# A layer's feed-forward: its first three output pairs as plain products of a low and a high token half, placed in a written order beside the making of their operands

## Chip, cores, metric

One core of one Trainium2 chip. The time is device microseconds of one execution; the figure for a kernel is the median of its runs.

## What is computed

A decoder layer on 512 tokens of width 2048: a modulated RMS norm, one projection into a short convolution and an attention group, an output projection with a gated residual, a second modulated norm, a feed-forward of width 8192 with squared ReLU, a gated residual, a last norm. The change lies between the end of the output projection and the first pairs of the feed-forward:

```
x = x + g1 * ([RMSNorm(y_conv) | RMSNorm(y_nsa)] @ W_out)
h = RMSNorm(x) * (1 + scale2) + shift2
x = x + g2 * (relu(h @ W1)^2 @ W2)
return RMSNorm(x)
```

## The kernel before, in words

Everything is float32. A product in full precision is three TensorE matmuls of operands that are each split into a high and a low part of the type float32r: high by high, high by low, low by high (`mm3`, lines 92 to 95). ScalarE makes the high part by a copy, VectorE the low part by a subtraction (`split`, `hilo`, `tsplit`). A weight block is 128 x 1024; `hilo` (line 794) is thus one operation of 1024 columns on each of the two engines.

**The end of the output projection.** Eight blocks of `w_oa2` are made into `kept` (lines 829 to 840). `late_out(hf)` (line 843) multiplies them with one half of the tokens (256 columns): eight products of 24 matmuls, and after each the gated residual (line 809), a square on ScalarE (line 804) and its sum on VectorE (line 805). Low half and high half together are 16 late products.

**Tokens.** When the sums of a half are complete, `row_norm` and `row_bcast` (lines 168 to 183) make the reciprocal root of each token and spread it over the partitions, with two small matmul steps. `normed` (line 872) multiplies by it on VectorE (tile xr) and modulates on ScalarE (line 880). `low_tokens` splits the low half into the token tiles B1 and B2; `high_tokens(q)` takes the high half, forms with the low half the differences and sums of a Strassen scheme of seven products, and splits those (tiles tk).

**The feed-forward.** The first matrix has 32 output pairs (256 columns of W1 each); a pair has four blocks, a11, a21, a22, a12. `ff1(p)` (line 966) makes seven products in place of eight: `operands` (line 913) forms the four sums of blocks that the scheme needs (VectorE, 1024 columns each, lines 917, 918, 930, 932), and splits seven operands; each product is `run`: 24 matmuls of 256 columns. The results are added up on VectorE and ScalarE, and seven tiles of the next layer's operands are split and stored to DRAM through the GpSimd queue (lines 1001 to 1014). The seven products in order are B1, U6, T5, B2, T7, B3, T4. Two of them, B1 and B2, need low tokens alone. So `ahead` (line 957) makes B1 and B2 for pairs 0 to 2 early, between the steps of `high_tokens`; these six products are left out when the pair's turn comes, which leaves five a pair.

**Order.** The program is written with a scheduler that may move instructions of one engine past each other where data allow it; `pin` keeps those passed to it in written order while `pinned[0]` is True. In the kernel before that is so only in the first part (lines 98 to 406). In the stretch of the change the scheduler chooses the order. Each engine then runs its own list strictly in that order, waiting at semaphores for others.

**Buffers that matter.** Three tiles `hl` for split blocks; six `rw` for raw blocks, loaded by the SyncE queue; three `gt` and one `gb` for what is stored to DRAM, each free again only when its stores have landed; eight PSUM banks; five small `t` tiles.

## Time and profile before

| | |
|---|---|
| median of 3 runs | 2225.86 us (2222.83 to 2229.16) |
| profiled execution, its own time | 2224.18 us |
| its span, first to last instruction | 2222.4 us |
| granted TensorE clock, mean | 0.982 |

The profile is of one execution. PE is TensorE's matmuls, PEld its weight loads, DVE VectorE, ACT ScalarE, POOL GpSimd, SP SyncE. A row of the timeline has the start and the length in microseconds, the engine, the line, the operation, the tiles written and read with their shape, a count, and in brackets the idle time ahead of it and what ended it. A row of busy time by stage has the window, its width, the busy time of each engine with the number of instructions, the granted clock, the DMA share and GB/s.

### The profile page before, as it was taken

To read this page: it belongs to the slowest core of one execution; us is meant where nothing else is said; L and a number is where in the kernel's file an instruction comes from. 1 tells how busy PE (TensorE), PEld (TensorE's weight loads), DVE (VectorE), ACT (ScalarE), POOL (GpSimd) and SP (SyncE) were. 2 spreads that over 40 slices of the span, in tenths; PEclk is the share of its full clock that TensorE was granted. 3 is DMA by queue.
4 is the path that set the end of the run, shared out by engine and by line. 5 is a ranking of instruction groups with operands and counts; after the bars stand their busy time and mean duration, and the time that the engine had idled before them with its cause. 6 is when DMAs were issued, how large, how long until landed. Compare 5 with 4: busy or idle time off the path is not lost.

```text
span 2222.4 us, 37638 instructions
## 1 busy us (share of the span) xinstructions
PE 2133.1 (96%) x14942; PEld 1971.6 (89%) x14942; DVE 1918.5 (86%) x2998; ACT 1008.6 (45%) x1468; POOL 193.6 (9%) x366
## 2 busy tenths in 40 slices
PE   6999999999999999799999999999899999999996
PEld 4777778898777779799999999999899999999996
DVE  8889988877496687999999999999898999999996
ACT  4432333223354425565666655666333333333353
POOL 0000000000000001021111111113111011001100
PEclk8999999999999999799999999999999999999998
DMA  8985687864211174276665666658865366356432
GB/s 351 336 321 187 235 302 269 348 233 162 81 39 67 48 286 164 83 235 209 199 203 189 198 209 204 204 187 285 298 237 210 141 237 237 129 214 247 168 118 95
DMA packets 143985, 453.62 MB, mean 204 GB/s; under 512 B 15809, under 2 KB 20161, under 8 KB 143809
## 3 DMA queue, kind: packets, MB, share of 16 engines
q1 hardware_dynamic: 92192, 323.27, 40.6%
q0 software_dynamic: 51616, 127.95, 17.3%
q8 instruction: 117, 1.92, 0.3%
q14 instruction: 60, 0.48, 0.1%
HBM read 383.00 MB, written 68.16 MB: 203 GB/s over the span
## 4 chain that ended last, share of the span: by engine, by line
PE 77%; DVE 13%; ACT 5%; DMA 3%; issue 2%; SPq 0%; POOL 0%; DVEq 0%; ACTq 0%; POOLq 0%
PE pf L95 19%; PE pf L93 19%; PE pf L94 18%; PE ps L95 5%; PE ps L94 5%; PE ps L93 5%; DVE scr L134 3%; DVE wl L84 2%; DVE hl L796 1%; ACT wh L83 1%; PE pw L94 1%; PE pw L95 1%; PE pw L93 1%; PE pt L714 1%; PE pv L93 1%
## 5 line engine op out<-in xcount | busy, mean ns | idle before, releaser
L93 PE MATMUL pf<-tk,hl 128*128 128x256 f32 x3576 | 1008.8, 282 | 11.5 <-ACT hl L795 9.1
L95 PE MATMUL pf<-tk,hl 128*128 128x256 f32 x3576 | 1006.2, 282 | 11.4 <-DVE hl L796 11.4
L94 PE MATMUL pf<-tk,hl 128*128 128x256 f32 x3576 | 1007.7, 282 | 1.3 <-DVE tk L867 1.3
L93 PEld LDWEIGHTS pf<-tk,hl 128*128 128x128 f32 x3576 | 678.7, 190 | 14.9 <-ACT hl L795 12.0
L95 PEld LDWEIGHTS pf<-tk,hl 128*128 128x128 f32 x3576 | 677.6, 190 | 14.0 <-DVE hl L796 13.9
L94 PEld LDWEIGHTS pf<-tk,hl 128*128 128x128 f32 x3576 | 677.5, 189 | 1.6 <-DVE tk L867 1.6
L795 ACT ACTIVATE hl<-rw 128x1024 fp32r<-128x1024 f32 x264 | 278.9, 1056 | 299.2 <-PE pf L95 253.2
L796 DVE TENSOR_TENSOR hl<-rw,hl 128x1024 fp32r<-128x1024 f32 x264 | 321.9, 1219 | 28.8 <-ACT hl L795 28.6
L795 ACT ACTIVATE hl<-sg 128x1024 fp32r<-128x1024 f32 x189 | 200.3, 1061 | 269.2 <-PE pf L95 245.6
L796 DVE TENSOR_TENSOR hl<-sg,hl 128x1024 fp32r<-128x1024 f32 x189 | 230.6, 1221 | 41.9 <-ACT hl L795 41.5
L134 DVE SCALAR_TENSOR_TENSOR scr<-wa,cs 128x1024 bf16<-128x1024 f32 x176 | 210.9, 1220 | 5.9 <-DMA wa<-in_w_ada 5.6
L83 ACT ACTIVATE wh<-raw 128x1024 fp32r<-128x1024 f32 (+1 forms) x105 | 110.9, 1060 | 223.6 <-PE ps L94 105.1
L84 DVE TENSOR_TENSOR wl<-raw,wh 128x1024 fp32r<-128x1024 f32 (+1 forms) x105 | 128.6, 1225 | 57.8 <-ACT wh L83 56.8
L870 DVE TENSOR_TENSOR sg<-sg,rw 128x1024 f32<-128x1024 f32 x126 | 153.6, 1219 | 0.9
L95 PE MATMUL ps<-h_m,wl 128*128 128x512 f32 x360 | 142.8, 397 | 2.4 <-DVE wl L84 2.4
L93 PE MATMUL ps<-h_m,wh 128*128 128x512 f32 x360 | 142.6, 396 | 1.8 <-DVE part L384 1.0
L94 PE MATMUL ps<-h_m,wh 128*128 128x512 f32 x360 | 141.8, 394 | 0.0
L1044 DVE SCALAR_TENSOR_TENSOR x<-pf,mod,x 128x256 f32<-128x256 f32 x256 | 120.1, 479 | 15.3 <-PE pf L95 12.3
L93 PE MATMUL ps<-h,wh 128*128 128x512 f32 x280 | 113.4, 405 | 12.6 <-ACT wh L83 8.9
L95 PE MATMUL ps<-h,wl 128*128 128x512 f32 x280 | 113.6, 406 | 2.4 <-DVE wl L84 2.4
L94 PE MATMUL ps<-h,wh 128*128 128x512 f32 x280 | 113.0, 404 | 0.0
L1010 POOL DMA_DIRECT2D g<-gt x192 | 101.0, 532 | 86.5 <-DVE gt L867 81.6
(314 smaller groups left out, 2972.6 us busy)
## 6 DMA issues: line engine op xcount, KB each, us to landing
rw<-in_w_f SPq DMA_DIRECT2D x262, 512.0 KB, 4.4
wa<-in_w_ada SPq DMA_DIRECT2D x176, 512.0 KB, 5.9
tk<-g POOLq DMA_DIRECT2D x114, 512.0 KB, 8.9
g<-gt POOLq DMA_DIRECT2D x192, 256.0 KB, 5.0
raw<-in_w_conv SPq DMA_DIRECT2D x32, 512.0 KB, 6.2
g<-gb POOLq DMA_DIRECT2D x36, 256.0 KB, 2.3
raw<-in_w_kv SPq DMA_DIRECT2D x16, 512.0 KB, 5.4
raw<-in_w_cv SPq DMA_DIRECT2D x16, 512.0 KB, 4.3
```

Of the source, the lines that this page charges most:

```text
L83: pin(nc.scalar.activation(wh[:, :cols], raw[:, :cols], AF.Copy))
L84: pin(nc.vector.tensor_tensor(out=wl[:, :cols], in0=raw[:, :cols], in1=wh[:, :cols].bitcast(F32), op=OP.subtract))
L93: pin(nc.tensor.matmul(ps, lh, rh, start=start, stop=False, skip_group_check=more))
L94: pin(nc.tensor.matmul(ps, lh, rl, start=False, stop=False, skip_group_check=more))
L95: pin(nc.tensor.matmul(ps, ll, rh, start=False, stop=stop, skip_group_check=more))
L134: pin(nc.vector.scalar_tensor_tensor(out=scr, in0=w, scalar=1.0, in1=cs[i].rearrange("p a b -> p (a b)"), op0=OP.mult, op1=OP.mult, accum_ ...
L714: nc.tensor.transpose(pt[:, r * P:(r + 1) * P], probs[b, r][:, kb * P:(kb + 1) * P], ident)
L795: nc.scalar.activation(dst[0], src, AF.Copy)
L796: nc.vector.tensor_tensor(out=dst[1], in0=src, in1=dst[0].bitcast(F32), op=OP.subtract)
L870: nc.vector.tensor_tensor(out=dst, in0=x, in1=y, op=op)
L1010: nc.gpsimd.dma_start(out=gd[p // 4][idx[j]][p % 4 // 2][:, p % 2], in_=g[:, j])
L1044: nc.vector.scalar_tensor_tensor(out=xm, in0=src, scalar=gate, in1=xm, op0=OP.mult, op1=OP.add)
```

## The change

In the whole kernel, calls are wrapped in `pin`, which changes nothing where `pinned[0]` is False. Between the making of `kept` and pair 3 it is now True, and the order is written out:

- The late products get half a bank each. Each residual is issued one product later.
- `norm_steps`, `low_tokens` and `high_tokens` are generators that yield after each piece the VectorE time that its author gives it, or None where the next piece belongs between two products.
- `product` issues one product, then the making of the operands listed for it, then pieces from the generators until their clock has caught up with 2.82 a product.
- Pairs 0 to 2 are computed without Strassen sums: four blocks by two token halves, 24 products of the same size where there were 21. `plan` lists them: the low half for pairs 0, 1, 2 (A11 and A21 with B1, A12 and A22 with B2), then the high half for pairs 2, 0, 1 (tokens T5 and B3). A product of the high half goes on in the other half of the same bank, whose low result was copied (`snapshot`). The high half of T5 is now x_high - x_low, so the accumulated high half plus the copy gives the result.
- `makes` says after which product an operand is made, `stay` which operands are kept for the second half; 19 blocks are split in these pairs, where there were 21.
- `outcome(p)` is the end of a pair: Relu, Square, the sums for the next layer and the stores, again as a generator. What is still waiting after product 24 is issued in full before pair 3 begins.
- In pairs 3 to 31 the tokens of T5 have the other sign, so one block of seven is made negated (`hilo(..., minus)`).

The diff, without lines that only gain `pin`:

```
-    def hilo(dst, src):
-        nc.scalar.activation(dst[0], src, AF.Copy)
-        nc.vector.tensor_tensor(out=dst[1], in0=src, in1=dst[0].bitcast(F32), op=OP.subtract)
+    def hilo(dst, src, minus=False):
+        if minus:
+            pin(nc.scalar.activation(dst[0], src, AF.Copy, scale=-1.0))
+            pin(nc.vector.scalar_tensor_tensor(out=dst[1], in0=src, scalar=-1.0, in1=dst[0].bitcast(F32),
+                                               op0=OP.mult, op1=OP.subtract))
+        else:
+            pin(nc.scalar.activation(dst[0], src, AF.Copy))
+            pin(nc.vector.tensor_tensor(out=dst[1], in0=src, in1=dst[0].bitcast(F32), op=OP.subtract))
         return dst
...
-    pm = [bankf() for _ in range(8)]
-    def late_out(hf):
+    late = {}
+    def late_product(hf, i):
+        if i % 2 == 0:
+            late[hf, i] = bankf()
+        ps = late[hf, i - i % 2][:, halves[i % 2]]
+        wh, wl = kept[i]
+        for k in range(8):
+            s = slice(k * P, (k + 1) * P)
+            mm3(ps, wh[:, s], wl[:, s], mixa[k][:, 0, halves[hf]], mixa[k][:, 1, halves[hf]], k == 0, k == 7)
+    def late_residual(hf, i):
         c = halves[hf]
-        for i in range(8):
-            wh, wl = kept[i]
-            for k in range(8):
-                s = slice(k * P, (k + 1) * P)
-                mm3(pm[i][:, c], wh[:, s], wl[:, s], mixa[k][:, 0, c], mixa[k][:, 1, c], k == 0, k == 7)
-            residual(pm[i], 8 + i, c)
-            if i % 2:
-                j = 4 + i // 2
-                nc.gpsimd.dma_start(out=x1d[j][:, :, c], in_=x1[j][:, :, c])
+        residual(late[hf, i - i % 2][:, halves[i % 2]], 8 + i, c)
+        if i % 2:
+            j = 4 + i // 2
+            pin(nc.gpsimd.dma_start(out=x1d[j][:, :, c], in_=x1[j][:, :, c]))
...
+    def norm_steps(hf):
+        total = bankf()
+        yield None
+        for t in range(2):
+            pin(nc.tensor.matmul(total[:, t:t + 1], sacc[:, (2 * hf + t) * P:(2 * hf + t + 1) * P], ones[:, 0:1],
+                                 start=True, stop=True))
+        rs = small.tile([P, NQ], F32, name="rs")[:, :2]
+        pin(nc.scalar.activation(rs, total[:, :2], AF.Sqrt, scale=1.0 / D, bias=eps))
+        yield 0.0
+        pin(nc.vector.reciprocal(rs, rs))
+        dg = temp([P, 2, P], name="dg")
+        pin(nc.vector.tensor_tensor(out=dg, in0=ident[:, None, :].to_broadcast([P, 2, P]),
+                                    in1=rs[:, :, None].to_broadcast([P, 2, P]), op=OP.mult))
+        yield 0.6
+        ps = bankf()
+        yield None
+        pin(nc.tensor.matmul(ps[:, :HT], ones, dg.rearrange("p a b -> p (a b)"), start=True, stop=True))
+        pin(nc.scalar.activation(r2[:, halves[hf]], ps[:, :HT], AF.Copy))
+        yield 0.0
     def low_tokens():
-        row_norm(bankf, sacc, D, r2, 0, 2)
+        for i in (B1, B2):
+            for q in range(4):
+                tok[i][q] = tslot()
+        def parts(i, u, kp):
+            dst = tok[i][kp // 2][:, kp % 2]
+            return dst, x1[kp][:, u, LO]
...
+        for kp in range(9):
+            if kp < 8:
+                normed(kp, 0)
+                yield 0.6
+            if kp:
+                dst, x = parts(B1, 0, kp - 1)
+                pin(nc.vector.tensor_tensor(out=dst[:, 1], in0=x, in1=dst[:, 0].bitcast(F32), op=OP.subtract))
+                yield 0.35
+            if kp < 8:
+                for u, i in ((0, B1), (1, B2)):
+                    dst, x = parts(i, u, kp)
+                    pin(nc.scalar.activation(dst[:, 0], x, AF.Copy))
+        for kp in range(8):
+            dst, x = parts(B2, 1, kp)
+            pin(nc.vector.tensor_tensor(out=dst[:, 1], in0=x, in1=dst[:, 0].bitcast(F32), op=OP.subtract))
+            yield 0.35
+    def high(dst, t):
+        pin(nc.scalar.activation(dst[:, :, 0], t, AF.Copy))
+    def low(dst, t):
+        pin(nc.vector.tensor_tensor(out=dst[:, :, 1], in0=t, in1=dst[:, :, 0].bitcast(F32), op=OP.subtract))
+    def high_tokens():
+        t5 = {}
+        for q in range(6):
+            if q < 4:
+                for j in range(2):
+                    normed(2 * q + j, 1)
+                    yield 0.6
+            if q > 1:
+                low(tok[T5][q - 2], t5.pop(q - 2))
+                for j in range(2):
+                    dst = tok[B3][q - 2][:, j]
+                    pin(nc.vector.tensor_tensor(out=dst[:, 1], in0=x1[2 * q - 4 + j][:, 1, HI],
+                                                in1=dst[:, 0].bitcast(F32), op=OP.subtract))
+                yield 1.3
+            if 0 < q < 5:
+                t5[q - 1] = temp((P, 2, HT), name="t5")
+                tok[T5][q - 1], tok[B3][q - 1] = tslot(), tslot()
+                for j in range(2):
+                    x = x1[2 * q - 2 + j]
+                    sub(t5[q - 1][:, j], x[:, 0, HI], x[:, 0, LO])
+                    pin(nc.scalar.activation(tok[B3][q - 1][:, j, 0], x[:, 1, HI], AF.Copy))
+                high(tok[T5][q - 1], t5[q - 1])
+                yield 0.7
+        due = []
+        for q in range(4):
+            xs2 = [x1[2 * q], x1[2 * q + 1]]
+            ts = [temp((P, 2, HT), name="tn") for _ in range(3)]
+            for n, i in enumerate((T7, U6, T4)):
+                for j, x in enumerate(xs2):
+                    if i == T7:
+                        sub(ts[0][:, j], x[:, 0, HI], x[:, 1, HI])
+                    else:
+                        sub(ts[n][:, j], x[:, n - 1, LO], ts[n - 1][:, j])
+                yield 0.7
+                for m in ((0,), (), (1, 2))[n]:
+                    tok[(T7, U6, T4)[m]][q] = tslot()
+                    high(tok[(T7, U6, T4)[m]][q], ts[m])
+                    due.append((tok[(T7, U6, T4)[m]][q], ts[m]))
+                if len(due) > (1 if q else 0) and due[0][1] is not ts[n]:
+                    low(*due.pop(0))
+                    yield 0.6
+        for d in due:
+            low(*d)
+            yield 0.6
...
-        skip = only is not None
-        if not skip:
-            yield hilo(hl_tile(), a11)
-        else:
-            yield None
+        yield hilo(hl_tile(), a11)
         yield hilo(hl_tile(), s2)
-        yield hilo(hl_tile(), s1)
-        if not skip:
-            yield hilo(hl_tile(), a12)
-        else:
-            yield None
+        yield hilo(hl_tile(), s1, minus)
+        yield hilo(hl_tile(), a12)
         sub(a21, a21, a11, OP.add)
         yield hilo(hl_tile(), a21)
         sub(s2, s2, a12, OP.add)
         yield hilo(hl_tile(), s2)
         yield hilo(hl_tile(), a22)
...
-    def run(ps, w, toks, first, last, base=0, n=8):
+    def run(ps, w, toks, first, last, base=0, n=8, c=LO):
-            mm3(ps[:, :HT], wh[:, s], wl[:, s], t[:, 0], t[:, 1], first and k == 0, last and k == n - 1, True)
+            mm3(ps[:, c], wh[:, s], wl[:, s], t[:, 0], t[:, 1], first and k == 0, last and k == n - 1, True)
...
-    pre = {}
-    def snapshot(p):
-        p1 = ffp.tile([P, HT], F32, name="p1", bufs=3)
-        nc.scalar.activation(p1, pre[p][0][:, :HT], AF.Copy)
-        pre[p].append(p1)
-    def ahead(p, i):
-        w = hilo(hl_tile(), raw_blob(a["w_f1"][p, 0 if i == B1 else 3]))
-        if i == B1:
-            pre[p] = [bankf()]
-        run(pre[p][0], w, tok[i], i == B1, True)
-        if i == B1:
-            snapshot(p)
+    def store(p, g, i):
+        pin(nc.gpsimd.dma_start(out=gd[p // 4][i][p % 4 // 2][:, p % 2], in_=g))
...
-    late_out(0)
-    low_tokens()
-    late_out(1)
-    ahead(0, B1)
-    row_norm(bankf, sacc, D, r2, 2, 4)
-    ahead(1, B1)
-    high_tokens(0)
-    ahead(2, B1)
-    high_tokens(1)
-    ahead(0, B2)
-    high_tokens(2)
-    ahead(1, B2)
-    ahead(2, B2)
-    high_tokens(3)
-    for p in range(32):
+            pin(nc.gpsimd.dma_start(out=dst[p % 4 // 2][:, p % 2], in_=g))
+    A11, A21, A22, A12 = range(4)
+    NP = 3
+    plan = []
+    for p in range(NP):
+        for b, i, u in ((A11, B1, 0), (A21, B1, 1), (A12, B2, 0), (A22, B2, 1)):
+            plan.append((p, b, i, u, 0, i == B1))
+    for p, order in ((2, (A21, A12, A22, A11)), (0, (A21, A22, A11, A12)), (1, (A11, A21, A12, A22))):
+        begun = set()
+        for b in order:
+            u = int(b in (A21, A22))
+            plan.append((p, b, T5 if b in (A11, A21) else B3, u, 1, u not in begun))
+            begun.add(u)
+    makes = {0: (3,), 1: (4,), 2: (5,), 3: (6,), 5: (7,), 6: (8,), 7: (9,), 8: (10,), 9: (11,), 13: (15,),
+             14: (18,), 15: (19,), 16: (20,), 19: (21,), 20: (22,), 21: (23,)}
+    stay = {12: 9, 13: 10, 14: 11, 16: 1, 17: 3}
+    made = {}
+    waiting = []
+    blocked = {}
+    clock = [0.0, 0.0]
+    def make(n):
+        p, b = plan[n][:2]
+        if n == 1:
+            dst = [ffp.tile([P, 1024], F32R, name="sg", bufs=2) for _ in range(2)]
+        elif n == 3:
+            dst = [ffp.tile([P, 2, 2, HT], F32R, name="gt", bufs=3).rearrange("p a b c -> p (a b c)")
+                   for _ in range(2)]
+        else:
+            dst = hl_tile()
+        made[n] = hilo(dst, raw_blob(a["w_f1"][p, b]))
+    def between():
+        for g in list(waiting):
+            if blocked.pop(g, False):
+                while (c := next(g, 0.0)) is None:
+                    pass
+    def fill():
+        while clock[1] < clock[0] - 0.3:
+            g = next((g for g in waiting if not blocked.get(g)), None)
+            if g is None:
+                return
+            waiting.remove(g)
+            try:
+                c = next(g)
+            except StopIteration:
+                continue
+            waiting.append(g)
+            if c is None:
+                blocked[g] = True
+            else:
+                clock[1] += c
+    def product(task, makes, later):
+        between()
+        task()
+        clock[1] = max(clock[1], clock[0])
+        clock[0] += 2.82
+        for f in makes:
+            f()
+            clock[1] += 1.15
+        for f, cost in later:
+            f()
+            clock[1] += cost
+        fill()
+    pinned[0] = True
+    later = []
+    for i in range(8):
+        product(lambda: late_product(0, i), (), later)
+        later = [(lambda i=i: late_residual(0, i), 0.8)]
+    for f, _ in later:
+        f()
+    later = []
+    def chain():
+        yield from norm_steps(0)
+        yield from low_tokens()
+    waiting.append(chain())
+    for i in range(8):
+        n = {1: 0, 2: 2, 7: 1}.get(i)
+        product(lambda: late_product(1, i), () if n is None else (lambda: make(n),), later)
+        later = [(lambda i=i: late_residual(1, i), 0.8)]
+    banks2, snaps = {}, {}
+    spare = slot(name="snap")
+    def snapshot(n):
+        p, b, i, u, hf, first = plan[n]
+        snaps[p, u] = spare[:, (2 * p + u) * HT:(2 * p + u + 1) * HT] if p < 2 \
+            else ffp.tile([P, HT], F32, name="p1", bufs=3)
+        pin(nc.scalar.activation(snaps[p, u], banks2[p, u][:, LO], AF.Copy))
+    def outcome(p):
+        xy = ffp.tile([P, 1024], F32, name="rw", bufs=6)
+        x, y = [xy[:, h * T:(h + 1) * T].rearrange("p (a b) -> p a b", a=2) for h in range(2)]
+        for u in range(2):
+            pin(nc.scalar.activation(x[:, u], banks2[p, u][:, LO], AF.Relu))
+        pin(nc.scalar.activation(x, x, AF.Square))
+        for u in range(2):
+            sub(y[:, 1 - u], snaps[p, u], banks2[p, u][:, HI], OP.add)
+        yield 0.8
+        pin(nc.scalar.activation(y, y, AF.Relu))
+        pin(nc.scalar.activation(y, y, AF.Square))
+        g = ffp.tile([P, 2, 2, HT], F32R, name="gt", bufs=3)
+        tsplit(g, x)
+        for j, i in enumerate((B1, B2)):
+            store(p, g[:, j], i)
+        yield 0.6
+        zv = ffp.tile([P, 1024], F32, name="rw", bufs=6)
+        z, v = [zv[:, h * T:(h + 1) * T].rearrange("p (a b) -> p a b", a=2) for h in range(2)]
+        sub(z[:, 0], x[:, 0], y[:, 1])
+        sub(z[:, 1], y[:, 1], y[:, 0])
+        sub(v[:, 0], z[:, 0], y[:, 0], OP.add)
+        sub(v[:, 1], x[:, 1], v[:, 0])
+        yield 1.4
+        for t, idx in ((z, (T5, T7)), (v, (U6, T4))):
+            g = ffp.tile([P, 2, 2, HT], F32R, name="gt", bufs=3)
+            tsplit(g, t)
+            for j in range(2):
+                store(p, g[:, j], idx[j])
+            yield 0.6
+        g = ffp.tile([P, 2, HT], F32R, name="gb", bufs=1)
+        split(g, y[:, 0])
+        store(p, g, B3)
+        yield 0.35
+    def pair_product(n):
+        p, b, i, u, hf, first = plan[n]
+        if hf == 0 and first:
+            banks2[p, u] = bankf()
+        run(banks2[p, u], made[stay.get(n, n)], tok[i], first, True, c=halves[hf])
+    def after_sums():
+        yield from norm_steps(1)
+        yield from high_tokens()
+    for n in range(len(plan)):
+        product(lambda: pair_product(n), [lambda m=m: make(m) for m in makes.get(n, ())], later)
+        later = []
+        if n == 0:
+            waiting.append(after_sums())
+        if plan[n][2] == B1:
+            later.append((lambda n=n: snapshot(n), 0.0))
+        if n >= 12 and n % 4 == 3:
+            later.append((lambda p=plan[n][0]: waiting.insert(0, outcome(p)), 0.0))
+    for f, _ in later:
+        f()
+    while waiting:
+        clock[0] += 10.0
+        fill()
+    pinned[0] = False
+    for p in range(NP, 32):
```

More of the change, by code (lines that the diff above doesn't have):

```diff
@@ L170, in row_norm @@
         for t in range(t0, t1):
-            nc.tensor.matmul(total[:, t:t + 1], square[:, t * P:(t + 1) * P], ones[:, 0:1],
-                             start=True, stop=True)
+            pin(nc.tensor.matmul(total[:, t:t + 1], square[:, t * P:(t + 1) * P], ones[:, 0:1],
+                                 start=True, stop=True))
         row_bcast(bank, total[:, t0:t1], width, dst[:, t0 * P:t1 * P])
@@ L754, in hybrid_layer @@
     tot = small.tile([P, NQ], F32, name="tot")
-    nc.vector.tensor_tensor(out=tot, in0=ssq[:, 0], in1=ssq[:, 1], op=OP.add)
+    pin(nc.vector.tensor_tensor(out=tot, in0=ssq[:, 0], in1=ssq[:, 1], op=OP.add))
     ra = accum("rc")
@@ L824, in hybrid_layer @@
     for i in range(8):
-        residual(pm[i], i, whole)
+        residual(pm[i][:, whole], i, whole)
         if i % 2:
-            nc.gpsimd.dma_start(out=x1d[i // 2], in_=x1[i // 2])
+            pin(nc.gpsimd.dma_start(out=x1d[i // 2], in_=x1[i // 2]))
     kept = []
@@ L915, in operands @@
+    def operands(raw, minus=False):
         a11, a21, a22, a12 = raw
@@ L1043, in update @@
         gate = ngate[:, m:m + 1] if neg else col(M_G2, m)
-        nc.vector.scalar_tensor_tensor(out=xm, in0=src, scalar=gate, in1=xm, op0=OP.mult, op1=OP.add)
+        pin(nc.vector.scalar_tensor_tensor(out=xm, in0=src, scalar=gate, in1=xm, op0=OP.mult, op1=OP.add))
     def final(m, c):
```

260 lines of the change are left out of this document (114 added, 146 removed).

## The prediction, made before the result was known

> **What bounds the kernel now.** I read the page first: engine shares, then the 40 slices.
>
> ```profile
> span 2222.4 us, 37638 instructions
> PE 2133.1 (96%) x14942; PEld 1971.6 (89%) x14942; DVE 1918.5 (86%) x2998; ACT 1008.6 (45%) x1468; POOL 193.6 (9%) x366
> ...
> PE   6999999999999999799999999999899999999996
> ...
> DVE  8889988877496687999999999999898999999996
> ...
> PEclk8999999999999999799999999999999999999998
> ```
>
> TensorE (PE) is the bound almost everywhere; the slice at 889 to 944 us, a 7 among nines, is the exception, and its granted clock is 0.7 too. That is the stretch which the change rewrites. Next, busy time by stage:
>
> ```profile
> 850.00:880.00 30.00, 30.00 (x253) 29.87 (x252) 20.91 (x41) 12.63 (x29) 3.40 (x5) 1.00 0.49 168
> 880.00:900.00 20.00, 18.13 (x150) 17.67 (x148) 16.48 (x36) 14.85 (x35) 2.03 (x3) 1.00 0.25 93
> 900.00:920.00 20.00, 12.98 (x67) 11.78 (x66) 18.39 (x40) 15.23 (x30) 0.00 (x0) 0.71 0.15 53
> 920.00:940.00 20.00, 15.18 (x85) 14.01 (x85) 18.98 (x32) 9.07 (x15) 0.00 (x0) 0.69 0.25 80
> 940.00:960.00 20.00, 18.99 (x159) 18.61 (x158) 19.92 (x29) 12.39 (x18) 3.72 (x7) 1.00 0.76 232
> 960.00:980.00 20.00, 19.51 (x160) 18.75 (x159) 19.79 (x30) 14.22 (x22) 4.75 (x9) 1.00 0.83 255
> 980.00:1000.00 20.00, 20.00 (x172) 20.00 (x171) 19.26 (x27) 12.18 (x19) 3.70 (x7) 1.00 0.61 198
> ```
>
> After the width come PE, PEld, DVE, ACT, POOL, then clock. From 900 to 980 us VectorE (DVE) is full and PE is not: 67 matmuls in a stage where 172 fit. The waits of 870 to 985 us name the operand that is late, the low part of a weight block:
>
> ```profile
> PE pf L95 <- DVE hl L796: 8.5, 6, 3.1
> PE pf L93 <- ACT hl L795: 3.1, 3, 1.1
> ```
>
> So DVE work is what this stretch has too much of. Its size in PE's own unit, a product (24 matmuls of 256 columns), comes from four rows: the first late matmul, and three uses of a pair's last product.
>
> ```profile
> 840.04 0.28 PE L93 MATMUL pf<-mixa,hl 128*128 128x256 f32 x1
> ...
> 996.80 0.42 DVE L870 TENSOR_TENSOR gx<-pf,p 128x256 f32<-128x256 f32 x1
> ...
> 1234.32 0.42 DVE L870 TENSOR_TENSOR gx<-pf,p 128x256 f32<-128x256 f32 x1
> ...
> 1254.12 0.42 DVE L870 TENSOR_TENSOR gx<-pf,p 128x256 f32<-128x256 f32 x1
> ```
>
> A steady pair of seven products takes 19.80 us, 2.83 each. From 840.04 to the end of pair 3 (996.80 less 0.3, a matmul's own length, 996.5) there are 16 late products, 6 early, 15 of pairs 0 to 2 and 7 of pair 3: 44, or 124.5 us of 156.5. PE loses **31.9 us**. From there it runs without a gap, so the end of pair 3 is where I compare.
>
> **The change part by part.** The built order of the new kernel matches the old outside this stretch, except that one block of seven in the pairs is made negated (same widths, same engines; nothing while DVE has room and PE has none):
>
> ```profile
> 1100.00:1200.00 100.00, 100.00 (x851) 100.00 (x850) 91.74 (x122) 61.81 (x87) 17.94 (x35) 1.00 0.63 200
> ```
>
> The order lists 72 more matmuls, three products: **+8.5 us** of PE. DVE loses 14 operations of 1024 columns (12 Strassen sums, two remakes) and nine of 256; ScalarE (ACT) loses two of 1024 and gains three of 256. Spacing back to back, from runs of equal operations (duration of all less duration of one, over the rest):
>
> ```profile
> 943.01 2.35 DVE L796 TENSOR_TENSOR hl<-sg,hl 128x1024 fp32r<-128x1024 f32 x2
> ...
> 872.59 2.49 DVE L876 TENSOR_TENSOR xr<-x,rc 128x512 f32<-128x512 f32 x4
> ...
> 898.50 1.42 DVE L870 TENSOR_TENSOR t<-x 128x256 f32<-128x256 f32 x4
> ...
> 880.48 0.88 DVE L809 SCALAR_TENSOR_TENSOR x<-pf,mod,x 128x256 f32<-128x256 f32 x2
> ...
> 941.74 2.01 ACT L795 ACTIVATE hl<-sg 128x1024 fp32r<-128x1024 f32 x2 [4.35 <-DVE sg L870]
> ...
> 904.93 2.08 ACT L880 ACTIVATE x<-xr,mod,aff 128x256 f32<-128x256 f32 x4
> ...
> 900.08 1.14 ACT L866 ACTIVATE tk<-t 128x512 fp32r<-128x512 f32 x2
> ...
> 874.31 0.71 ACT L89 ACTIVATE tk<-x 128x256 fp32r<-128x256 f32 x2
> ```
>
> DVE: 1.14 (1024), 0.60 (512), 0.34 (256), 0.40 (residual). ACT: 0.95 (1024), 0.50 (modulate), 0.52 (512), 0.31 (256). DVE sheds 14 x 1.14 + 9 x 0.34 = 19 us. But every instruction of the stretch now stands in written order, so an engine whose next instruction waits does nothing else. I walked the new order by hand, each start being the later of its engine and its operands, a hand-over taking 0.03. PE's waits, place by place:
>
> *Late products.* The second needs its block's low part:
>
> ```profile
> 843.81 1.22 DVE L796 TENSOR_TENSOR hl<-rw,hl 128x1024 fp32r<-128x1024 f32 x1
> ...
> 845.08 0.39 PE L95 MATMUL pf<-mixa,hl 128*128 128x256 f32 x1 [0.41 <-DVE hl L796]
> ```
>
> In the old order PE puts ten matmuls of other products in between; now it stands from 843.1 to 845.1: 2.0. A norm sum and a spread add 0.6 (the spread's row below is 0.59 long). The 16 products end at 887.9, as now:
>
> ```profile
> 887.62 0.28 PE L93 MATMUL pf<-tk,hl 128*128 128x256 f32 x1
> ```
>
>
> *Low tokens.* The products of the three pairs are numbered 1 to 24 here. Now the tokens are one ACT run, eight rounds of 1.6 us (two modulates, two high parts), squares afterwards:
>
> ```profile
> 873.31 1.09 ACT L880 ACTIVATE x<-xr,mod,aff 128x256 f32<-128x256 f32 x2 [1.62 <-DVE xr L876]
> ...
> 885.52 0.71 ACT L89 ACTIVATE tk<-x 128x256 fp32r<-128x256 f32 x2
> 886.13 2.25 ACT L804 ACTIVATE sq<-x 128x256 f32<-128x256 f32 x7
> ...
> 894.14 0.59 PE L192 MATMUL pf<-dg,ones 128*128 128x256 f32 x2
> ...
> 894.77 0.38 ACT L182 ACTIVATE rc<-pf 128x256 f32<-128x256 f32 x1 [1.56 <-PE pf L192]
> ```
>
> In the new order the low sums follow the first high product (867.5), the diagonal waits behind a weight block and a residual with its square, the spread comes at 873.6, and its copy 0.63 later behind one more square: r2 at 874.9 and, after another residual, the first modulate at 876.9. In every second round DVE stands on a residual's square, which ACT does after two modulates, and the next token's multiply is behind it: 2.1 us a round, last B1 low part at 893.6. PE wants it from 887.9: product 1 ends 3.3 late. Product 2's block is made behind the tokens: 1.5. The high-half sums stand ahead of product 3 and need the last residuals, which lie behind those blocks: 2.0 and 0.2. The spread needs a diagonal that DVE reaches behind another block: 1.4. Sum **8.4**; product 4 starts at 904.8.
>
> *High tokens.* Four multiplies, then eight modulates (4.0), three high parts (1.2) and four modulates (2.0) stand on ACT ahead of the block of product 8: its high part is ready at 916.5, its low at 917.8; PE wants it at 916.1. DVE stands from 912.0 to 916.5. Products 9, 10 and 11 each need a block behind a T5 difference, its high part on ACT, and the low part back on DVE: ready 922.6, 927.5 and 932.3. PE waits 1.5 + 2.0 + 2.0 + 2.1 = **7.6**. Products 12 to 24 then have their blocks in time but for 1.1 and 0.4: product 24 ends at 973.35.
>
> *The tail.* Pair 3's first block (ACT and DVE) is queued behind the whole outcome of pair 1, which needs product 24: two Relus and a Square (0.9), the sums y, Relu and Square of y (1.9), the split of x, then z, v and y, each into a buffer whose two earlier stores must have landed:
>
> ```profile
> g<-gt POOLq DMA_DIRECT2D x192, 256.0 KB, 5.0
> ```
>
> The splits of pair 0 end at 972.6 and 973.4, two issues of 0.53 each, 5 us to land: 978.2 and 979.3. The block's high part is ready at 981.25, its low at 982.5. PE stands 973.4 to 981.3. What it does then, rows after waits of 3 us show:
>
> ```profile
> 916.54 0.58 PE L95 MATMUL pf<-tk,hl 128*128 128x256 f32 x1 [3.08 <-DVE hl L796]
> ...
> 907.34 0.41 PE L94 MATMUL pf<-tk,hl 128*128 128x256 f32 x1
> 907.55 0.41 PE L95 MATMUL pf<-tk,hl 128*128 128x256 f32 x1
> ```
>
> Starts 0.21 apart instead of 0.118 (19.80 / 168): half clock. So 22 matmuls take 4.7, to 987.2; then the order sets one matmul of T5 ahead of the rest of U6, and T5's block waits on ACT for the copy of pair 3's first product: 1.5 more. Against 7 x 2.83 from 973.35, pair 3 ends at 1005.5: **12.35** lost (10.5 at full clock).
>
> The Trainium skill, "TensorE: Matmul & The Clock Gate", section "Part 1: The HAM clock gate", says that an idle window of about 3.4 us halves the clock and a busy one restores it. By it the tail, 8 us idle, must start cold, as the rows above already make it; it would also start product 1's successors cold if the low-token wait counts as idle, which is rival three.
>
> Sum of waits: 2.0 + 0.6 + 8.4 + 7.6 + 1.5 + 12.35 = 32.45, against 31.9 now; with the 8.5 of added products **+9.0 us**. The 19 us of DVE work that go return as waits in order. The profiled execution took 2224.18 (span 2222.4), so 2233.2; the median of the runs lies 1.7 above it, so **2235**. DMA is not late: blocks are loaded up to six buffers ahead, and land in
>
> ```profile
> rw<-in_w_f SPq DMA_DIRECT2D x262, 512.0 KB, 4.4
> ```
>
>
> **The rivals.** One: *DVE's relief reaches PE*; faster. If the queues interleave better than my walk (hand-overs that I made serial overlap), the waits of low and high tokens and the 1.5 go, 17.5 us, while the tail stays: 9.0 - 17.5 = -8.5, **2217**. It decides from the point where block 8 is ready before 916. For it: DVE is busy 18 to 20 of 20 us in the old stretch, and sheds 19. Against it: the high part of block 8 stands behind 15 ACT operations in the order, whatever DVE does. Two: *only the high-token waits go*, -7.6: **2227**, no change; for it, ACT is busy only 9 to 15 of 20 us there. Three: *the clock falls already at the low tokens*. Between 889.7 and 893.6 PE would have nine matmuls, 1.1 us of work in 3.9. Products 2 to 4 at half clock cost 24 x 0.095 = 2.3 each, less the 3.4 of waits that this covers, +3.5; if it recurs at products 8 to 11, up to +7 more: 2239 to 2246. For it: clock 0.71 and 0.69 in today's thin stage; against it, 880 to 900 keeps 1.00 at 18.1 of 20 busy. That the change leaves the order as it was is excluded by the built order.
>
> **How the numbers follow.** Forecast 0.48 (own range 2229 to 2240), rival one 0.13, two 0.20, three 0.19. A measurement here tells about 0.3%, 6.7 us, from no change. Faster is rival one, 0.13; within are rival two and a fifth of the forecast, 0.30; slower the rest, 0.57. The range 2219 to 2244 leaves out most of rival one below and the top of three.
>
> **What would show it.** In the new profile: a PE gap near 973 to 981 us ended by ACT's block of pair 3, then matmuls 0.21 apart; PE waits on the low part of blocks at about 917, 922, 927 and 932; DVE idle around 912 to 916; the first token product paced by ACT. Pair 3's last product, now 996.5, at about 1005. The forecast is wrong if PE is fed from 900 to 970 or if the tail is short.

## The result and the profile after

The changed kernel takes 2242.4 us (median of 4 runs, 2240.55 to 2243.37), the kernel before 2224.35 (4 runs): ratio **1.0075**, 95% interval 1.0063 to 1.0088. It is 18 us slower, where the sum had 9.0, and above the forecast's own range of 2229 to 2240. The profiled execution took 2243.37, its span 2241.6.

The page of the changed kernel, engine shares and then slices:

```profile
span 2241.6 us, 37738 instructions
...
PE 2143.8 (96%) x15014; PEld 1981.4 (88%) x15014; DVE 1900.6 (85%) x2975; ACT 1007.6 (45%) x1469; POOL 193.6 (9%) x366
...
PE   6999899999999999879999999999899999999997
...
DVE  8889988876496686789999999999889999999996
...
PEclk7999999999999999899999999999999999999998
```

PE has its 72 matmuls more, DVE its 18 us less. The hole in the PE row has become longer (8 and 7 where one 7 stood), and DVE is no longer full beside it: its slices from 841 us on read 6, 7, 8, then nines. So this stretch no longer has too much DVE work; it has engines that wait for each other. The stages (columns as before: PE, PEld, DVE, ACT, POOL, clock, DMA) say where:

```profile
880.00:900.00 20.00, 17.06 (x129) 15.93 (x128) 10.89 (x24) 14.55 (x37) 1.35 (x2) 0.92 0.16 62
900.00:920.00 20.00, 18.92 (x128) 17.91 (x129) 15.13 (x28) 11.63 (x23) 0.68 (x1) 0.83 0.42 147
920.00:940.00 20.00, 14.72 (x108) 14.11 (x107) 10.95 (x19) 13.02 (x25) 0.00 (x0) 0.91 0.24 79
940.00:960.00 20.00, 19.05 (x161) 18.84 (x160) 18.23 (x38) 10.77 (x16) 0.00 (x0) 1.00 0.13 51
960.00:980.00 20.00, 20.00 (x167) 19.75 (x167) 16.48 (x32) 12.93 (x24) 4.79 (x9) 1.00 0.60 179
980.00:1000.00 20.00, 8.02 (x49) 7.32 (x48) 13.40 (x19) 9.18 (x15) 6.85 (x13) 0.74 1.05 319
```

From 880 to 940 no engine is full, and from 980 to 1000 PE issues 49 matmuls where 172 fit. The waits of PE from 840 to 1020 us (us in total, times, longest) give the names:

```profile
PE pf L93 <- ACT hl L800: 10.3, 1, 10.3
PE pf L93 <- ACT snap L1164: 3.4, 2, 3.2
PE pf L93 <- ACT p L1164: 2.9, 2, 1.9
PE pf L95 <- DVE hl L801: 2.3, 2, 1.8
PE pf L94 <- DVE tk L928: 2.0, 1, 2.0
```

Before, the largest was the low part of blocks, by DVE, 8.5 us. Now it is one wait of 10.3 on ACT (pair 3's first block) and 6.3 on the copies of low results, which the forecast did not have at all. The ends of the stretch, and PE's stand ahead of pair 3, from the timeline (the last row is the use of pair 3's last product):

```profile
842.25 0.28 PE L93 MATMUL pf<-mixa,hl 128*128 128x256 f32 x1
...
980.48 0.28 PE L95 MATMUL pf<-tk,hl 128*128 128x256 f32 x1
991.09 0.58 PE L93 MATMUL pf<-tk,hl 128*128 128x256 f32 x1 [10.33 <-ACT hl L800]
...
1016.14 0.42 DVE L879 TENSOR_TENSOR gx<-pf,p 128x256 f32<-128x256 f32 x1
```

From the first late matmul to pair 3's end are 173.9 us, where the kernel before has 996.80 - 840.04 = 156.8: **17.1 more**, where the sum had 9.0. What follows to the end of the span, 1225.5 us, is as long as before (1225.6); the other 2.2 of the longer span lie ahead of the late products. This length of the stretch is used below beside the ratios, because the start of the late products lies between 837.47 and 843.51 in the profiles of kernels that have the same program up to there.

### The profile page after: what moved, and what is told of

It is laid out like the page before. It is cut to its first block, busy times and chain, and to the rows that moved or that the text cites. A ratio compares the mean times of both kernels' runs of the same rounds, so it can differ in the third digit from the quotient of the medians.

```text
span 2241.6 us, 37738 instructions
## 1 busy us (share of the span) xinstructions
PE 2143.8 (96%) x15014; PEld 1981.4 (88%) x15014; DVE 1900.6 (85%) x2975; ACT 1007.6 (45%) x1469; POOL 193.6 (9%) x366
## 3 DMA queue, kind: packets, MB, share of 16 engines
q0 software_dynamic: 51616, 127.95, 17.1%
## 4 chain that ended last, share of the span: by engine, by line
PE 73%; DVE 7%; ACT 3%; DMA 2%; issue 2%; SPq 0%; POOL 0%; DVEq 0%; ACTq 0%; POOLq 0%
PE pf L95 18%; PE pf L93 18%; PE pf L94 18%; PE ps L95 4%; PE ps L94 4%; PE ps L93 4%; DVE hl L801 1%; PE pw L94 1%; PE pw L95 1%; PE pw L93 1%; PE pt L714 1%; ACT x L889 1%; DVE wl L84 1%; PE pv L93 1%; ACT hl L800 1%
## 5 line engine op out<-in xcount | busy, mean ns | idle before, releaser
L800 ACT ACTIVATE hl<-rw 128x1024 fp32r<-128x1024 f32 x269 | 283.7, 1056 | 291.9 <-PE pf L95 257.3
L801 DVE TENSOR_TENSOR hl<-rw,hl 128x1024 fp32r<-128x1024 f32 x269 | 327.6, 1218 | 45.2 <-ACT hl L800 45.2
L800 ACT ACTIVATE hl<-sg 128x1024 fp32r<-128x1024 f32 x151 | 160.2, 1061 | 255.5 <-PE pf L95 244.2
L801 DVE TENSOR_TENSOR hl<-sg,hl 128x1024 fp32r<-128x1024 f32 x151 | 184.3, 1221 | 42.8 <-ACT hl L800 42.6
L879 DVE TENSOR_TENSOR sg<-sg,rw 128x1024 f32<-128x1024 f32 x120 | 146.2, 1218 | 0.9
```

The lines of the kernel that those rows point to most:

```text
L800: pin(nc.scalar.activation(dst[0], src, AF.Copy))
L801: pin(nc.vector.tensor_tensor(out=dst[1], in0=src, in1=dst[0].bitcast(F32), op=OP.subtract))
L879: pin(nc.vector.tensor_tensor(out=dst, in0=x, in1=y, op=op))
```

## The experiments

The theory after the result: the order written by hand is what costs; ACT and DVE work through one long chain from the late products to pair 3, and PE waits for it. The main rival: the three added products and the clock cost the time, whatever the order. Two more causes were open: the shared banks of the late products, and the stores that must land before pair 3 begins.

| label | ratio to before, 95% interval | median us (before on its chip) | stretch us |
|---|---|---|---|
| the change | 1.0075, 1.0063 to 1.0088 | 2242.4 (2224.35) | 173.9 |
| e1_sched | 0.9982, 0.9972 to 0.9991 | 2222.31 (2226.75) | 152.6 |
| e2_tail | 1.0047, 1.0032 to 1.0062 | 2237.26 (2226.75) | 168.1 |
| e3_resid | 1.0091, 1.0076 to 1.0106 | 2246.57 (2226.75) | 180.2 |
| e4_snap | 1.0084, 1.0067 to 1.0101 | 2245.51 (2226.75) | 173.9 |
| e9_both | 0.9946, 0.9933 to 0.9960 | 2213.12 (2225.53) | 143.7 |
| e10_gtbuf | 1.0081, 1.0067 to 1.0094 | 2243.34 (2225.53) | 175.7 |
| e5_late | 1.0128, 1.0112 to 1.0144 | 2254.1 (2225.53) | 186.8 |
| e6_less_high | 1.0083, 1.0069 to 1.0097 | 2243.28 (2225.53) | 173.6 |
| e11_banks | 1.0062, 1.0047 to 1.0077 | 2239.82 (2226.61) | 172.6 |
| e12_banks_fill | 1.0053, 1.0038 to 1.0068 | 2237.41 (2226.61) | 169.8 |
| e13_land | 1.0044, 1.0027 to 1.0061 | 2235.69 (2226.61) | 170.0 |
| e14_sched_less | 0.9923, 0.9909 to 0.9938 | 2209.47 (2226.61) | 140.1 |

**The order undone (e1_sched).**

```
-    pinned[0] = True        (ahead of the late products)
```

> The new products without Strassen sums, but the stretch is handed back to the scheduler, which orders each engine by its own model as in the kernel before; only the written order is undone. Theory (most of the loss beyond the 8.5 us of three added products is waiting in the written order, in the low tokens, at the snapshots and in the tail): the time moves by several us, either way, and the pattern of waits changes: the 10.3 us wait on pair 3's first block and the 2.1 us rounds of the low tokens look different. If the scheduler places better than the hand, 2225 to 2236; if worse, 2245 or more. Rival (the arithmetic itself costs the 18 us, by the added matmuls and by PE's clock in a thin stage, whatever the order): within 3 us of 2242.

It is 20 us faster than the change, better than the range expected of a good order, and 0.18% under the kernel before, with every product and every operand the same. The arithmetic is not the cause; the order is. One of the written order's waits stays, since the outcomes are still issued ahead of pair 3 in the program:

```profile
967.99 0.58 PE L93 MATMUL pf<-tk,hl 128*128 128x256 f32 x1 [6.90 <-ACT hl L800]
```

**The tail alone (e2_tail).** In `ff1`, once a product, and instead of the emptying ahead of pair 3:

```
+            if waiting and next(waiting[0], None) is None:
+                waiting.pop(0)
...
-    while waiting:
-        clock[0] += 10.0
-        fill()
```

> Pair 3 begins at once after product 24; the pieces of the outcomes that are still waiting are issued one at a time between its products instead of all ahead of them, and the scheduler has the order from product 24 on. Theory (PE's 10.6 us stand after product 24 is pair 1's outcome queued ahead of pair 3's first block on ACT and DVE, two of whose buffers wait for stores to land): the stand shrinks to 0 to 2 us, with it the cold start of about 2.5 us: 2230 to 2234. Rival one (the landing of the stores is the bound itself, since pair 3's own operands need it): gap 4 to 8 us, 2238 or more. Rival two (ACT and DVE have no room beside pair 3, so the outcome's work comes back as waits in pairs 3 and 4): 2238 to 2242, with new waits after 995 us.

The stretch is 5.8 shorter. The wait of 10.3 is gone, but smaller ones stand in pair 3, and half-speed matmuls with them (clock 0.83 from 980 to 1000); the three longest:

```profile
980.12 0.39 PE L93 MATMUL pf<-tk,hl 128*128 128x256 f32 x1 [1.50 <-ACT hl L800]
981.38 0.38 PE L95 MATMUL pf<-tk,hl 128*128 128x256 f32 x1 [0.76 <-DVE hl L801]
...
987.17 0.39 PE L93 MATMUL pf<-tk,hl 128*128 128x256 f32 x1 [1.42 <-ACT hl L800]
```

That lies between the theory and rival two: the queue was the cause of the stand, and part of the outcome's work comes back beside pair 3.

**Both (e9_both).** The two edits above together.

> Both edits that have gained, together: the stretch is handed back to the scheduler, and pair 3 begins at once after product 24 with the outcomes' pieces between its products. Theory (the waits of the written order and the queued outcome are separate terms): the scheduler's order (2222 with its 6.9 us stand before pair 3) loses most of that stand and of the half clock behind it, 5 to 9 us: 2213 to 2217, under the kernel before. Rival (ACT and DVE have no room beside pair 3, and the outcome comes back as waits of products): 2220 to 2223.

2213.1: 0.54% under the kernel before, as the theory had it, and the fastest kernel of this study apart from the one that leaves work out. Its stages and PE's waits from 840 to 1040 us:

```profile
900.00:920.00 20.00, 18.46 (x154) 18.05 (x153) 19.39 (x38) 19.05 (x38) 0.00 (x0) 1.00 0.33 106
920.00:940.00 20.00, 20.00 (x171) 20.00 (x170) 19.12 (x38) 11.78 (x19) 0.00 (x0) 1.00 0.15 54
940.00:960.00 20.00, 20.00 (x171) 20.00 (x171) 15.46 (x27) 12.75 (x21) 7.45 (x14) 1.00 0.94 289
960.00:980.00 20.00, 18.45 (x153) 17.94 (x152) 17.23 (x23) 11.73 (x17) 4.25 (x8) 1.00 0.84 253
```

```profile
PE pf L95 <- DVE hl L801: 3.4, 3, 1.5
PE pf L93 <- ACT snap L1165: 1.3, 1, 1.3
PE pf L94 <- DVE tk L943: 0.2, 1, 0.2
```

ACT and DVE are both at 19 of 20 from 900 to 920, where the written order left them at 11.6 and 15.1; PE has its work and a full clock. 47 products of 2.83 are 133.0 us, so of the stretch (143.7, less the 0.3 of a matmul's length) some 10 us are lost, against 31.9 before. So the same products and operands can run faster than the kernel before. That it is the saved DVE work which now reaches PE is the likely reason, but not shown by itself: this kernel differs from the one before in banks and in the pieces of the tail as well.

**The low tokens freed of residuals (e3_resid).** `later[:4]` of the high half's residuals with product 1, the other four with product 2.

> The residuals of the eight high late products, with their squares, are held back: four are issued with product 1 and four with product 2, so the low tokens no longer share ACT and DVE with them; the high sums start one product later. Theory (the low tokens run in rounds of 2.1 us because DVE stands on each residual's square in ACT's queue, and start late because the residual of an even product waits for the odd product in the same bank): rounds of 1.6 us, the low parts ready 6 to 7 us earlier, product 4 about 4 to 6 us earlier, no half clock at 898 to 908: 2234 to 2238. Rival (the rounds are bound by ACT itself, or what is won is given back at the high tokens, whose sums now wait for the late residuals): 2240 to 2244.

The rounds became 1.6 us, as expected, and the kernel slower (stretch +6.3). The copy of a low result, which product 3 needs, is now queued on ACT behind the squares:

```profile
902.79 0.42 ACT L809 ACTIVATE sq<-x 128x256 f32<-128x256 f32 x1 [0.94 <-DVE x L814]
903.12 0.36 ACT L1164 ACTIVATE snap<-pf 128x256 f32<-128x256 f32 x1
...
903.53 0.58 PE L93 MATMUL pf<-tk,hl 128*128 128x256 f32 x1 [10.42 <-ACT snap L1164]
```

The wait moved along the queue, and grew. The rival had it right that the gain is given back, though not where.

**The copy ahead of the block (e4_snap).** In `product`, copies are issued before the makings.

> The copy of a low result (snapshot) is issued ahead of the making of the next block on ACT instead of behind it; nothing else moves. Theory (products that go on in a bank wait for its copy, which stands behind a 0.95 us high part that itself waits for data: 3.20, 0.18, 1.90 and 0.95 us at products of the second low operand): these four waits go, but most of them hide waits for blocks that come next, so 1 to 3 us: 2239.5 to 2241.5. Rival one (they are covered by nothing: all 6.2 us are won): 2236. Rival two (the blocks are the bound, so the same time stands as waits on blocks' low parts): 2242.

No gain: the stretch is the same to 0.1 us, and the ratio is no lower. Waits on the copy fell from 6.3 to 5.0 and those on a block's low part rose from 2.3 to 3.5. This agrees with rival two: block and copy stand one behind the other on ACT, and both are late.

**Products left out, in either order (e6_less_high, e14_sched_less).**

```
+        if n in (14, 17, 19):
+            return
```

> Products 15, 18 and 20 of 24 are left out (a third of the added and old work of the high half in pairs 2 and 0, whose results are then incomplete); every making of an operand, copy and outcome stays. They stand where PE has been fed without waits. Theory (an added product costs its own 2.83 us there, the 8.5 us term of the sum): 2233 to 2235. Rival (ACT and DVE, with blocks, token sums and outcomes, are as long as PE in this stage, so that fewer products turn into waits): 2237 to 2241.

> Products 15, 18 and 20 are left out again (pairs 2 and 0 are then incomplete in the high half), now with the scheduler's order and pair 3 begun at once, the version that ran 2213. Theory (there PE is the bound, 171 matmuls in each 20 us, so that a product costs its own 2.83; in the written order the queues of ACT and DVE are the bound, and the same three products cost nothing): 2204 to 2207. Rival (the making of operands and outcomes is as long as the products in any order): 2210 to 2213.

In the written order, 8.5 us less work for PE gain 0.3 in the stretch. PE waits instead, at 952.8, 969.8 and in the tail:

```profile
969.78 0.38 PE L93 MATMUL pf<-tk,hl 128*128 128x256 f32 x1 [4.30 <-ACT hl L800]
...
991.29 0.58 PE L93 MATMUL pf<-tk,hl 128*128 128x256 f32 x1 [8.54 <-ACT hl L800]
```

So even where PE showed 20.00 of 20, ACT's and DVE's chain was as long, and the theory's 8.5 falls. With the scheduler's order the same three products are worth more. The stretch shows 3.6 (143.7 to 140.1), but its end is read from an instruction of DVE, which in e14 is late itself. Two pairs further on, the same instruction of pair 5 comes 183.6 us after the first late matmul (840.10) in e9 and 178.4 after it (841.58) in e14. These are e9's row and e14's:

```profile
1023.72 0.42 DVE L879 TENSOR_TENSOR gx<-pf,p 128x256 f32<-128x256 f32 x1
```

```profile
1019.96 0.41 DVE L879 TENSOR_TENSOR gx<-pf,p 128x256 f32<-128x256 f32 x1
```

That is 5.2, and the ratios give 5.1, with intervals that just overlap. It lies between theory and rival: more than half of the products' own time, but not all of it. PE's waits on blocks grow from 3.4 us in e9 to 6.1 in e14, so part of the gain returns as waits there too.

**A landing taken away (e10_gtbuf, e13_land).** First pair 1's z and v into buffers of the tokens' pool; then z there, v and the last y into small ones.

> The written order as it is; only the two buffers into which pair 1's z and v are split come from another pool, so that their splits need not wait for the stores of pair 0 to land. Theory (4.8 us of the 10.6 us stand before pair 3 are that landing: 3.83 and 1.01 of ACT's waits): the stand shrinks to 5.5 to 6.5, the cold start stays: 2237 to 2239. Rival one (the sums of the outcome are what takes the time, and the landing is beside them): 2241 to 2243. Rival two (a shorter stand also spares the half clock): 2234 to 2236.

> The written order; the splits of pair 1's z, v and last y go to buffers that no store holds (z to the one free large buffer, v and y to small ones, v in two halves), so that none of them waits for a store to land. Theory (the landing adds to the outcome's own sums, which end at 985.7 us, and pair 3's block then follows 3 us earlier): the stand shrinks from 10.3 to 7 to 7.5, 2239 to 2240.5. Rival one (all of the 4.84 us of ACT's waits on landings come back): 5.5, 2237 to 2238.5. Rival two (the landing is beside another wait of the same length): 2242 to 2244.

In e10 PE's stand before pair 3 did fall to the theory's length, but a second one of the same length followed. Its pool had one buffer free, and v's split waited for z's own stores, so one wait took the other's place (PE's timeline, then ACT's):

```profile
984.96 0.58 PE L93 MATMUL pf<-tk,hl 128*128 128x256 f32 x1 [5.85 <-ACT hl L800]
...
996.14 0.58 PE L93 MATMUL pf<-tk,hl 128*128 128x256 f32 x1 [5.74 <-ACT hl L800]
```

```profile
990.91 0.63 ACT L875 ACTIVATE tk<-rw 128x512 fp32r<-128x512 f32 x1 [6.00 <-DMA g<-tk]
```

e13 took the landing away. The waits of ACT in the changed kernel, and PE's restart in e13:

```profile
987.38 0.63 ACT L875 ACTIVATE gt<-rw 128x512 fp32r<-128x512 f32 x1 [3.83 <-DMA g<-gt]
989.01 0.63 ACT L875 ACTIVATE gt<-rw 128x512 fp32r<-128x512 f32 x1 [1.01 <-DMA g<-gt]
```

```profile
982.66 0.58 PE L93 MATMUL pf<-tk,hl 128*128 128x256 f32 x1 [6.76 <-ACT hl L800]
```

10.33 became 6.76, the stretch is 3.9 shorter. The theory said 7 to 7.5; it was a little more. (By the ratio the gain is 0.31%, with an interval that holds 3.9 us; this profile also begins its late products 4.8 earlier.) By the profiles the landing is worth under 4 of the 10.3; the outcome's own work is the rest.

**Filling the first stand, and banks (e5_late, e11_banks, e12_banks_fill).** e5 issues the first high late product behind the first low one. e11 gives each late product a bank of its own; e12 does both.

```
+        if i == 1:
+            product(lambda: late_product(1, 0), (), later)      (e5, e12)
...
-        ps = late[hf, i - i % 2][:, halves[i % 2]]
+        ps = late[hf, i][:, :HT]                                 (e11, e12)
```

> The first late product of the high half is issued right after the first of the low half, so that PE has work while the second block's low part is made; the low sums come one product later and the high half has seven left. Theory (the chain of low norm, low tokens and B1's low parts sets product 4, not PE, and it now starts 1 us later, 2.8 less the 1.8 stand): no gain, 2242 to 2244, PE's wait on the tokens longer by what is won before. Rival (PE's stand of 1.8 us, and the half clock of about 2 us after it where it comes, are paid in full): 2238 to 2240.5.

> The written order as it is, but each late product has a bank of its own instead of half of one. Theory (an even product's residual waits for the odd product in the same bank, which delays the low tokens by 2.4 us, and from there ACT's and DVE's queues carry the delay to the end of the stretch): first modulate about 2.4 us earlier, product 4 about 2 us earlier, 2239.5 to 2241. Rival (the late start of the tokens has another cause, the norm's own chain): 2242 to 2243.5. If the eight banks are then short at the first products, a wait on a residual appears there, and the time is 2243 or more.

> A bank of its own for each late product, and the first late product of the high half right after the first of the low half. Theory (the 7.7 us stand that this filler brought is a bank shared by two products: the next product writes the half beside the one whose residual, issued before it, stands behind the blocks' making on DVE): that stand is gone, and the time is that of own banks alone within 1.5 us, since the tokens and not PE set product 4. Rival one (the stand was not the bank's): 2250 or more again. Rival two (PE's first stand of 1.8 us is paid in full, so filling it gains on top of the banks): 2 us or more under own banks alone.

e5 met neither: it is 12.9 slower in the stretch. PE stands 7.71 us, for a residual that DVE reaches behind its blocks (PE's and DVE's timelines):

```profile
855.41 0.55 PE L93 MATMUL pf<-mixa,hl 128*128 128x256 f32 x1 [7.71 <-DVE x L814]
```

```profile
854.79 0.48 DVE L814 SCALAR_TENSOR_TENSOR x<-pf,mod,x 128x256 f32<-128x256 f32 x1
```

That residual reads the first half of a bank whose second half the next product writes. With own banks the stand is gone (e12). The same sharing, seen from DVE, delayed the changed kernel: an even product's residual waits for the odd product. The changed kernel, then e11:

```profile
881.32 0.48 DVE L814 SCALAR_TENSOR_TENSOR x<-pf,mod,x 128x256 f32<-128x256 f32 x1 [1.52 <-PE pf L95]
```

```profile
878.37 0.47 DVE L814 SCALAR_TENSOR_TENSOR x<-pf,mod,x 128x256 f32<-128x256 f32 x1
```

The Trainium skill, "PSUM — Partial Sum Buffer", section "PSUM bank collisions raise a hardware error", asks for guards by bank and quadrant, not by address. Both waits agree with it: they are between halves that share no element. e12 beats e11 by 2.8 in the stretch (2.0 by the ratios, whose intervals overlap). That leans to rival two, that PE's first stand is paid, but does not settle it: e11's profile has a half clock at the first products that not every execution has, and it accounts for some 1.5 of the 2.8 (next table). Without it the theory's "within 1.5" would hold.

How a shift at the start travels is seen in the same profiles, in us from the first late matmul of each (first modulate of a low token; product 7 begins, after its wait on a snapshot; pair 3 begins):

| kernel | modulate | product 7 | pair 3 begins |
|---|---|---|---|
| the change | 41.2 | 81.3 | 148.8 |
| e11_banks | 38.6 | 78.8 | 146.8 |
| e12_banks_fill | 36.8 | 77.0 | 144.6 |
| e6_less_high | 39.6 | 79.8 | 147.8 |
| e13_land | 41.1 | 81.3 | 145.2 |

2.5 us or 4.3 us earlier at the first token are as much earlier 40 us later, and 2.0 and 4.2 at pair 3. That is what a chain in order looks like. e6's row shows the same without an edit ahead of it. The change, e11 and e13 have matmuls at half clock in the first late products; e6 has none, and its first modulate comes 1.5 us earlier (39.6 for 41.2), as it does in e2, e4 and e10. So up to 1.5 us of a difference between such stretches is not the edit's: e6's 0.3 is then no gain, e4's equal stretch may be a small loss, and e2's 5.8 may hold some of it.

## Why the prediction was right in sign and short in size

- **Right: the order is what loses, and DVE's relief does not pay for it.** e1 shows it; the sum said that the 19 us of DVE work return as waits in order.
- **Right: the tail.** PE stands from 980.5 to 991.1 for pair 3's first block, then matmuls start 0.21 apart, as forecast for 973 to 981 (this profile begins the stretch 2.2 later). Also as forecast: the late products' stand (1.80 where 2.0 was said), low tokens paced by ACT in rounds of some 2.1, and DVE idle behind the high tokens (4.49 us, where 912.0 to 916.5 was said).
- **Short by 8.1 us, in these terms.** The walk is set 2.2 later, since the profile begins the stretch so. The norm sum of the low half stood 1.9 later than walked, at 871.62: mostly matmuls at half clock, 15 of them from 848.98 on at 0.095 each, 1.4, which belong to this execution and not to every one. The first modulate, walked to 879.1, came at 883.41, 4.3 late, of which 2.4 remain for the shared bank; e11 shows 2.5. To the end of product 24 (walked to 975.55, started its last matmul at 980.48) 0.6 were added. The tail's stand is 10.6 where 7.95 was walked: 2.7. Pair 3's own products took 0.55 more. The sum is 8.15.
- **The steps that failed.** "Late products": the walk took a residual to be free when its own product is, and did not see that a bank is waited for as a whole. "The tail": stores "5 us to land". The row was a median over the kernel; in this place, where the DMA share is 1.05 from 980 to 1000, they took longer (DMA view, 975 to 995 us, the column at the end; then the issues of pair 0's z and v on the timeline):

```profile
g<-gt POOLq DMA_DIRECT2D x12, 256.0 KB, 5.8
```

```profile
980.20 2.10 POOL L1021 DMA_DIRECT2D g<-gt  x4 [2.50 <-DVE gt L876]
```

The last of these four issues begins at 981.77, and ACT's split that waits for it starts at 989.01, 7.2 us later. Against the 5 of the walk that is some 2 of the 2.7; the rest was not taken apart.

- **Right sum by luck, wrong cause: products 8 to 11.** 7.6 were walked as waits on low parts of blocks. Measured are 6.2 on snapshots (the rounded rows above add up to 6.3), at products 7, 8, 11 and 12, and some 2 of half clock behind them. The copy of a low result stands on ACT behind the next block's making, a queue that the walk had not followed. e4 shows that the block would have been late anyway.
- **Wrong as a price: the 8.5 us of added products.** It is in the sum of the stretch, where waits and work must add up, but it is not what the three products cost. In the written order three products are worth 0.3 at most (e6), in the scheduler's order some 5 (e14). With fewer products, the waits would have been longer.
- **The rivals.** The result lies in the range of rival three, the clock falling at the low tokens. The clock did fall there (0.83 from 900 to 920), but it was not charged: product 24 ends only 0.6 later than the late start of the tokens explains, since ACT's and DVE's chain is the longer one. Rival one, DVE's relief reaching PE, priced at 2217, did not happen in this order; e9, in another order and without the tail, is 2213; rival one had kept the tail.

What remains open: why e5 loses 12.9 in the stretch where the stand is 7.7 (the rest was not taken apart), what the scheduler's order does in detail at the late products, and whether filling PE's first stand gains anything in an execution without the half clock.

## What to carry to other kernels

Where an order is written out by hand, a shorter list of work does not make the stretch shorter: find the one chain that runs through the in-order queues, and count what stands ahead of each instruction there, copies and residuals too. A busy engine is not yet the bound: take work away from it and see whether the end moves, as e6 did. And price a transfer by its neighbours at that place, not by its median.

## What the runs showed of the hardware

A half clock can come behind a short stand, in some executions only. In eight profiles (the change, e2, e3, e4, e6, e10, e11, e13) PE stands the same 1.8 us at the second late product; in three of them (the change, e11, e13) matmuls then start 0.21 apart for 3 us or more, in the other five none do so before the next stand. That the stand is the cause is not shown. The changed kernel's rows, 1.7 us after the stand:

```profile
848.80 0.38 PE L95 MATMUL pf<-mixa,hl 128*128 128x256 f32 x1
848.98 0.42 PE L93 MATMUL pf<-mixa,hl 128*128 128x256 f32 x1
849.19 0.41 PE L94 MATMUL pf<-mixa,hl 128*128 128x256 f32 x1
```

The Trainium skill, "TensorE: Matmul & The Clock Gate", section "Part 1: The HAM clock gate", has the window run freely, which would fit a fall in some executions only; but its idle window of about 3.4 us is longer than this stand, so by that rule no fall should have come here, and the cause stays open. After the 10.3 us of the tail the half clock came, as that rule and the prediction had it.
